# A hybrid encoder trunk on one core: blocks on TensorE, row-mode switches in the queue model, and new ranks

## The chip, the cores and the metric

One Trainium2 chip, one of its cores. The metric is the device time of one execution in microseconds (us). TensorE is called PE here, its weight loads PEld, VectorE DVE, ScalarE ACT, GpSimd POOL and SyncE SP, as in the profile. Smaller is better.

## The reference

Two layers over a sequence of 512 positions of width 1024, all in float32:

```
h = rmsnorm(x, g_attn[l]);  proj = h @ w_in[l]            # 1024 -> 2304 columns
# group A: 8 query heads, 2 key/value heads of 64, window +/-128, a learned sink logit per head
# group B: 4 differential heads, two q/k halves of 64, values of 128:
#          w = softmax(q1 k1) - lam * softmax(q2 k2);  yb = rmsnorm(w @ v) * (1 - lambda_init)
# every q/k head: rmsnorm over the head, then rotary
x = x + concat(ya, yb) @ w_out[l]
h = rmsnorm(x, g_ffn[l]);  gate, val = split(h @ w_up[l])  # 2 x 2816
gate = centred_dwconv(gate, conv_w[l], conv_b[l])          # width 3
x = x + (silu(gate) * val) @ w_down[l]
```

## The kernel before, in words

**Products.** A float32 product is made of three matmuls in a faster 32-bit format: each operand is split into a high part (a cast) and a low part (operand minus high part), and high x high, high x low and low x high are added up in PSUM. `mm3` makes such a triple product. Weights come from HBM in units of 512 KB or less (`wr`), ACT makes the high part (`wh`), DVE the low part (`wl`); there are two raw and three high and low buffers.

**A layer.** `filler` gives PE its large work in this order: projections of group A (`pj_akv`, `pj_aq`), of group B's first half (`pj_bq`, `pj_bk`), both value chunks (`pj_bv`), group B's second half, then the output projection: `out_pass` 0 for group A's part, `out_pass` 1 for group B's first half (`wo`, 512 columns wide), `out_last` twice for its second half (`wo`, 256 wide, one for each half of the positions), then the feed-forward part (`up`, `dn`). Beside it run the attention chains. Group A, for each of 8 tiles: scores `sc_a`, masked maximum and exponential (`so_a`), transposes `pt_a`, their split into `p_a`, product with the values `pv_a`. Group B, for each of 16 tiles named b(layer)_(head)_(query block): six score matmuls `sc_b` of 64 rows each, two heads' halves side by side; maximum `mx_b` on DVE over both; two exponentials `e_b` on ACT; reciprocal, factor and combination `e_b` on DVE; four transposes `wt_b`; split into `wh_b` and `wl_b`; twelve matmuls `yb` for two tiles of a head; after two heads the norm: square `sq_yb` (ACT), column sums `ss_yb` (PE), `rr_yb` (DVE, then a power on POOL), broadcast back by `rt_yb` (PE), `y_yb` (DVE), and the split `yh_b`, `yl_b` that the output projection reads. The scores have one double bank (`sc`), the projections two banks (`mm`).

**What sets the order.** Each piece of work is a generator, a *track*, which yields one operation at a time. `Machine.run` keeps a model of the engines: when each is free, when each operand is there (`Op.cost` has the assumed durations). Of all tracks' next operations it takes, engine by engine, those that could start within a hold time of the earliest, and of these the one with the smallest rank; that one is issued. So the order of the instructions on each engine is fixed when the program is built, and ranks decide between operations that are ready at about the same time: small ranks first, the filler 1000. Ranks touched here: the weight loads, casts and splits (`RK["w"]`, by whether 0, 1 or more units are ready), the evacuation of projection banks (3), q/k norm and rotary tracks of group A (5 and 6) and B (`RK["qkb"]`), the attention tiles of A (10 and up) and B (30 and up), the residual adds behind the output projection (4).

On the chip every engine works through its list in order; an instruction whose operand is late holds up all behind it. All instructions carry the line of the one helper that issues them (L230 before, L247 after), so they are told apart by the names of their tiles.

Of the kernel before, what the change touches and what calls it, by code (L numbers as in the profile page):

```python
# [35 lines left out]
NEAR = {"PE": 0.3, "POOL": 0.079}  # L36
LO_CUT = 2
# [4 lines left out]
RK = {"w": (1, 5, 49), "qkb": (7, 38)}  # L42


class Op:


    def __init__(self, eng, name, args, kw):
# [9 lines left out]
        self.port = False  # L58
        self.pitch, self.lag = self.cost(writes, reads)

    def cost(self, writes, reads):
        n = max([free_size(v) for v in writes[:1]] + [free_size(v) for v in reads])
        if self.eng == "PE":
            if self.name == "transpose" or free_size(writes[0]) <= P:
                return 0.111, 0.165
            n = free_size(writes[0])
            if reads[0].dtype == F32:
                return 4 * n / 2400 + 0.014, 0.165
            half = reads[0].partition_size() == HD
            return (n / 2400 + 0.0135) / (2 if half else 1), 0.165  # L70
# [19 lines left out]
        return 0.33, 0.0  # L90

# [38 lines left out]
class Machine:  # L130
# [3 lines left out]
    def __init__(self, nc):  # L134
        self.raw = {"PE": nc.tensor, "DVE": nc.vector, "ACT": nc.scalar, "POOL": nc.gpsimd, "SP": nc.sync}
# [11 lines left out]
    def tag(self, name, bufs):  # L147
        self.cap[name], self.live[name], self.slots[name] = bufs, 0, [0.0] * bufs

    def got(self, tag, tile_):  # L150
        self.live[tag] += 1
        assert self.live[tag] <= self.cap[tag], tag
        self.mem[tile_.tensor.name] = {"base": heapq.heappop(self.slots[tag])}
        return tile_

    def drop(self, tag, tile_):
        self.live[tag] -= 1
        m = self.mem.pop(tile_.tensor.name)
        heapq.heappush(self.slots[tag], max([m["base"]] + [t for k, v in m.items() if k != "base" for t in v[:2]]))
# [18 lines left out]

    def ready(self, op):
        t = 0.0  # L180
        for name, where in op.reads:
            m = self.mem.get(name)
            if m is None:
                continue
            t = max(t, m["base"])
            for k, (w, r, e) in m.items() if len(m) > 1 else ():
                pass
        return t
# [22 lines left out]
    def put(self, op, start):  # L211
        end = start + op.pitch + op.lag
# [18 lines left out]
        self.log.append((op.eng, start, op.pitch, op.name, op.writes[0][0]))  # L231
# [42 lines left out]
def kernel(  # L274
# [48 lines left out]
    def any_bank(name, tags):  # L323
        tag = min((t for t in tags if m.live[t] < m.cap[t]), key=lambda t: m.slots[t][0])
# [220 lines left out]
    def layer(l, norm):  # L545
# [70 lines left out]
        def qk_track(nm, tag, bank, tp, tab, dst, rq, rank, is_kv=False):  # L616
# [10 lines left out]
            m.spawn(3, go())  # L627

        def qk_out(nm, raw_t, sq_t, tp, tab_i, dst, rq, is_kv):
# [75 lines left out]
        def akv_done(tag, bank, tp):  # L705
            qk_track("ka", tag, bank, tp, 1, [v.unsqueeze(1) for v in ka], None, 5, True)

        def proj_a(i, tags):
            rq = lambda tp: rqa[:, 2 * tp:2 * tp + 2, 2 * i:2 * i + 2, :].rearrange("p t a b -> p t (a b)")
            yield from project(f"aq{i}", lambda tag, bank, tp: qk_track(  # L710
                f"qa{i}", tag, bank, tp, 0, qa[i], rq(tp), 6), tags)
# [14 lines left out]
        a_rank = {s: 10 + i for i, s in enumerate(a_seq)}  # L726
        b_rank = {s: 30 + i for i, s in enumerate(b_seq)}
        a_so = {}

        def a_scores(ip, qb):  # L730
# [9 lines left out]
            for i in range(2):  # L740
                yield m.room("sc")
                scp = new("sc", f"sc_{nm}_{i}")
                sc = (scp[:, 0], scp[:, 1])
                for j, (u, v) in enumerate(((0, 0), (0, 1), (1, 0))):
                    for g in range(2):
                        rs = slice(g * HD, (g + 1) * HD)
                        yield pe.matmul(sc[g][:, :n], lhsT=q[u][rs, i, qb * P:(qb + 1) * P],
                                        rhs=k[v][rs, kb0 * P:kb1 * P], start=j == 0, stop=j == 2)
# [42 lines left out]
        def a_values(ip, qb):  # L791
# [492 lines left out]
```

## Time and profile before

| | us |
|---|---|
| median of 3 runs (lowest, highest) | 1299.78 (1298.53, 1299.89) |
| the profiled execution | 1298.52 |
| its span, first to last instruction | 1296.7 |
| PE busy | 1241.0 |
| DVE, ACT, POOL busy | 756.3, 563.5, 216.9 |

The span runs through attention of layer 0 (to about 294 us), its feed-forward part (to about 650), attention of layer 1 (to about 930) and its feed-forward part. In the view by stretches, each row has the stretch, its length, and for every engine busy time and number of instructions; then the share of PE's full clock that was granted, the share of the DMA engines and GB/s. In a timeline row stand the start, the length, engine, line, operation, out<-in, and in brackets the idle time just before it with what ended it.

### The profile page before, as it was taken

The numbers are of one execution on the slowest core, as the hardware profiler recorded it, in microseconds if no ns is written. First come the engines' busy times: TensorE is split into PE (matmuls) and PEld (weight loads), VectorE is DVE, ScalarE is ACT, GpSimd is POOL, SyncE is SP. The second block draws the span as 40 slices with busy tenths as digits, with TensorE's granted clock in tenths as the row PEclk, the third lists the DMA queues.
The fourth block names the chain that finished last, engine by engine and source line by source line (L and its number), as shares of the span: only waits on it lengthen the run. The fifth ranks groups of instructions, "written<-read, shape, count | busy, mean of one in ns | idle before, by whom it ended". The sixth has DMA issues, their size and how long they took to land.

```text
span 1296.7 us, 17153 instructions
## 1 busy us (share of the span) xinstructions
PE 1241.0 (96%) x6644; PEld 1041.4 (80%) x6644; DVE 756.3 (58%) x1337; ACT 563.5 (43%) x979; POOL 216.9 (17%) x278
## 2 busy tenths in 40 slices
PE   8999899879999999999999999997799999999998
PEld 7987686667888888888898888775688888888887
DVE  6777677647555335554458777876555553355532
ACT  5467664425433223333445776444443332233321
POOL 2450052001111000110243503320011110011100
PEclk8999899879999999999999999998799999999999
DMA  6221121102332333332332211210133323332232
GB/s 206 66 66 34 33 66 51 48 1 84 100 95 91 94 105 98 98 98 75 104 106 66 66 50 50 66 49 18 33 98 97 98 78 98 114 94 94 91 106 91
DMA packets 33617, 102.93 MB, mean 79 GB/s; under 512 B 3968, under 2 KB 5248, under 8 KB 33536
## 3 DMA queue, kind: packets, MB, share of 16 engines
q1 hardware_dynamic: 33536, 101.84, 25.5%
q8 instruction: 52, 0.85, 0.3%
q14 instruction: 29, 0.24, 0.1%
HBM read 99.73 MB, written 2.10 MB: 79 GB/s over the span
## 4 chain that ended last, share of the span: by engine, by line
PE 86%; DVE 7%; ACT 3%; issue 2%; POOL 1%; DMA 0%; SPq 0%; ACTq 0%; DVEq 0%; POOLq 0%
PE up L230 36%; PE dn L230 18%; PE wo L230 5%; PE pj_aq L230 4%; PE pj_bq L230 3%; PE pj_bv L230 3%; PE pj_bk L230 2%; PE pv_a L230 2%; PE sc_b L230 2%; PE yb L230 2%; PE pj_akv L230 2%; PE sc_a L230 2%; PE pt_a L230 1%; DVE wl L230 1%; DVE mx_b L230 1%
## 5 line engine op out<-in xcount | busy, mean ns | idle before, releaser
L230 ACT CAST wh<-wr 128x1024 fp32r<-128x1024 f32 (+2 forms) x202 | 195.3, 967 | 391.4 <-PE up L230 176.6
L230 DVE TENSOR_TENSOR wl<-wr,wh 128x512 fp32r<-128x512 f32 (+3 forms) x248 | 230.6, 944 | 104.5 <-ACT wh L230 103.9
L230 PE MATMUL up<-nf_l,wh 128*128 128x512 f32 x704 | 274.1, 389 | 1.7 <-DVE nf_l L230 1.7
L230 PE MATMUL up<-nf_h,wh 128*128 128x512 f32 x704 | 274.3, 390 | 0.0
L230 PE MATMUL up<-nf_h,wl 128*128 128x512 f32 x704 | 274.1, 389 | 0.0
L230 PE MATMUL dn<-act,wh 128*128 128x512 f32 x704 | 216.8, 389 | 0.0
L230 PEld LDWEIGHTS up<-nf_l,wh 128*128 128x128 f32 x704 | 132.2, 188 | 29.7 <-DVE nf_l L230 2.4
L230 PEld LDWEIGHTS up<-nf_h,wh 128*128 128x128 f32 x704 | 132.2, 188 | 27.8 <-ACT nf_h L230 0.5
L230 PEld LDWEIGHTS dn<-act,wh 128*128 128x128 f32 x704 | 132.2, 188 | 27.4
L230 PEld LDWEIGHTS up<-nf_h,wl 128*128 128x128 f32 x704 | 132.2, 188 | 27.2
L230 POOL TENSOR_TENSOR cv<-cv,rb 128x512 f32<-128x512 f32 x44 | 57.3, 1302 | 525.8 <-ACT cv L230 525.8
L230 PE MATMUL dn<-act,wl 128*128 128x512 f32 x352 | 136.9, 389 | 0.0
L230 DVE TENSOR_TENSOR gp<-up,rb 128x512 f32<-128x512 f32 x44 | 30.5, 693 | 110.4 <-PE up L230 105.0
L230 DVE TENSOR_TENSOR cv<-cv,up 128x512 f32<-128x512 f32 x44 | 30.3, 688 | 90.0 <-POOL gp L230 81.4
L230 PEld LDWEIGHTS dn<-act,wl 128*128 128x128 f32 x352 | 66.1, 188 | 13.7
L230 DVE SCALAR_TENSOR_TENSOR cv<-gp,cols,cv 128x512 f32<-128x512 f32 x88 | 65.9, 749 | 7.0 <-ACT cv L230 2.5
L230 DVE TENSOR_TENSOR x<-x,dn 128x512 f32<-128x512 f32 x32 | 22.0, 688 | 74.1 <-PE dn L230 74.1
L230 ACT ACTIVATE e_b<-sc_b,mx_b,rqb 128x512 f32<-128x512 f32 x64 | 49.5, 776 | 34.1 <-DVE mx_b L230 31.6
L230 ACT ACTIVATE cv<-cv 128x512 f32<-128x512 f32 x44 | 27.8, 632 | 82.0 <-DVE cv L230 82.0
L230 DVE TENSOR_TENSOR x<-x,wo 128x512 f32<-128x512 f32 (+1 forms) x64 | 34.9, 551 | 18.2 <-PE wo L230 17.6
L230 DVE TENSOR_REDUCE mx_b<-sc_b 128x2 f32<-128x1024 f32 x32 | 39.1, 1221 | 10.8 <-PE sc_b L230 10.7
L230 ACT ACTIVATE so_a<-so_a,ng_a,rqa 128x256 f32<-128x256 f32 (+1 forms) x64 | 41.3, 650 | 3.6 <-DVE ng_a L230 3.5
(202 smaller groups left out, 2330.0 us busy)
## 6 DMA issues: line engine op xcount, KB each, us to landing
wr<-w_up SPq DMA_DIRECT2D x88, 512.0 KB, 3.6
wr<-w_in SPq DMA_DIRECT2D x34, 512.0 KB, 3.7
wr<-w_down SPq DMA_DIRECT2D x32, 384.0 KB, 3.0
wr<-w_down SPq DMA_DIRECT2D x32, 320.0 KB, 2.9
wr<-w_out SPq DMA_DIRECT2D x16, 512.0 KB, 3.7
x<-xT SPq DMA_DIRECT2D x8, 256.0 KB, 4.4
outT<-x SPq DMA_DIRECT2D x8, 256.0 KB, 2.0
prob_f<-w_in SPq DMA_DIRECT2D x8, 128.0 KB, 4.3
```

The costliest lines, as they stand in the source:

```text
L230: getattr(self.raw[op.eng], op.name)(*op.args, **op.kw)
```

## The change

It leaves every computation as it is, and does four things:

1. `Batch`: a group of PE operations that is yielded and issued as one, without others in between. The three matmuls of a triple product, the six scores of a tile (of A and of B), the transposes of a tile and the small products of the norm become such groups.
2. The model of PE: a matmul of 64 rows after one of 128 rows, or the other way round, now costs a switch (`SWITCH`: 0.2 into 64-row mode, 0.085 out of it); float32 products of 128 columns or fewer cost 0.222 and not 0.111; the time from an operand to PE goes from 0.3 to 0.2.
3. The ranks are set anew: group A's tiles from 10 to 39 and up, A's query track from 6 to 36, its key track from 5 to 2, group B's first half from 7 to 36 and second from 38 to 2, adds of the two output passes from 4 to 400, evacuations from 3 to 4, the norm of B four ranks behind its tile, weights with one unit ready from 5 to 28, with more from 49 to 400.
4. `LO_CUT` 2 to 1: the low parts of input and output projection weights are one operation of 1024 columns instead of two of 512.

```diff
-NEAR = {"PE": 0.3, "POOL": 0.079}
-LO_CUT = 2
+SWITCH = {True: 0.2, False: 0.085}
+NEAR = {"PE": 0.2, "POOL": 0.079}
+LO_CUT = 1
...
-RK = {"w": (1, 5, 49), "qkb": (7, 38)}
+RK = {"w": (1, 28, 400), "qkb": (36, 2), "x": 400, "xl": 4, "a": 39, "b": 30, "evac": 4, "qka": 36, "kv": 2,
+      "bn": 4, "nsq": 21, "av": -2, "bv": 0}
...
+class Batch:
+    def __init__(self, ops):
+        self.ops = ops
+        self.eng, self.port = "PE", False
+        self.reads = [r for o in ops for r in o.reads]
+        self.writes = [w for o in ops for w in o.writes]
+        self.pitch = sum(o.pitch for o in ops)
+        self.half = ops[0].half
...
     def put(self, op, start):
+        if isinstance(op, Batch):
+            for v in op.ops:
+                self.put(v, start)
+                start = self.free["PE"]
+            return
+        if op.eng == "PE" and op.half != self.half:
+            self.free["PE"] += SWITCH[op.half]
+            start += SWITCH[op.half]
+            self.half = op.half
...
     def mm3(acc, a, b, start, stop):
-        yield pe.matmul(acc, lhsT=a[0], rhs=b[0], start=start, stop=False)
-        yield pe.matmul(acc, lhsT=a[0], rhs=b[1], start=False, stop=False)
-        yield pe.matmul(acc, lhsT=a[1], rhs=b[0], start=False, stop=stop)
+        yield Batch([pe.matmul(acc, lhsT=a[0], rhs=b[0], start=start, stop=False),
+                     pe.matmul(acc, lhsT=a[0], rhs=b[1], start=False, stop=False),
+                     pe.matmul(acc, lhsT=a[1], rhs=b[0], start=False, stop=stop)])
...
-        a_rank = {s: 10 + i for i, s in enumerate(a_seq)}
-        b_rank = {s: 30 + i for i, s in enumerate(b_seq)}
+        a_rank = {s: RK["a"] + i for i, s in enumerate(a_seq)}
+        b_rank = {s: RK["b"] + i for i, s in enumerate(b_seq)}
...
+            ops = []
             for n, (u, v) in enumerate(((0, 0), (0, 1), (1, 0))):
                 for c in range(2):
                     rs = slice(c * HD, (c + 1) * HD)
-                    yield pe.matmul(scp[:, c], lhsT=q[u][rs, j, qb * P:(qb + 1) * P], rhs=k[v][rs, j, :],
-                                    start=n == 0, stop=n == 2)
+                    ops.append(pe.matmul(scp[:, c], lhsT=q[u][rs, j, qb * P:(qb + 1) * P], rhs=k[v][rs, j, :],
+                                         start=n == 0, stop=n == 2))
+            yield Batch(ops)
...
-                m.spawn(4, add_x(d, tag, acc, slice(0, S)))
+                m.spawn(RK["x"], add_x(d, tag, acc, slice(0, S)))
```

What this makes of the order, at three places. (In the names, `sc_b0_0_0` is the scores of layer 0, head 0, query block 0, and `yb0_1_1` the weighted values of layer 0, half 1, second pair of query blocks; `wo0_2_0_4` is the last output product of layer 0, first half of the positions, fifth block of rows. The number at a name's end tells buffers apart.)

PE, the scores of group B's first tile in layer 0, before:

```order
L230 MATMUL pv_a0_1_2_1829<-p_a0_1_2_1_1801,va0_89 128x512 x3
L230 MATMUL sc_b0_0_0_1834<-bkh0_0_677,bqh0_0_675 128x512
L230 MATMUL pv_a0_1_2_1829<-p_a0_1_2_2_1828,va0_89 128x512
L230 MATMUL sc_b0_0_0_1834<-bkh0_0_677,bqh0_0_675 128x512
L230 MATMUL sc_b0_0_0_1834<-bkl0_0_678,bqh0_0_675 128x512 x2
L230 MATMUL sc_b0_0_0_1834<-bkh0_0_677,bql0_0_676 128x512
L230 MATMUL pv_a0_1_2_1829<-p_a0_1_2_2_1828,va0_89 128x512 x2
L230 MATMUL sc_b0_0_0_1834<-bkh0_0_677,bql0_0_676 128x512
```

and now:

```order
L247 MATMUL pt_a0_1_2_2_1739<-ident_74,so_a0_1_2_1_1_1478 128x128
L247 MATMUL sc_b0_0_0_1762<-bkh0_0_677,bqh0_0_675 128x512 x2
L247 MATMUL sc_b0_0_0_1762<-bkl0_0_678,bqh0_0_675 128x512 x2
L247 MATMUL sc_b0_0_0_1762<-bkh0_0_677,bql0_0_676 128x512 x2
L247 MATMUL pv_a0_1_2_1757<-p_a0_1_2_0_1721,va0_89 128x512 x3
```

The six scores stand together; before, products of group A stood between them.

PE, the last norm of layer 0's attention, before:

```order
L230 MATMUL yb0_1_1_2963<-wh_b0_3_2_2999,vb0_1_1_1680 128x256
L230 MATMUL ss_yb0_1_1_3073<-unit_78,sq_yb0_1_1_3067 128x1 x4
L230 MATMUL rt_yb0_1_1_3081<-ident_74,rr_yb0_1_1_3078 128x128 x4
L230 MATMUL wo0_2_1_0_3089<-yh0_b1_2912,wh24_2622 128x256 x2
L230 MATMUL wo0_2_1_0_3089<-yh0_b1_2912,wl24_2641 128x256 x2
```

and now:

```order
L247 MATMUL wo0_2_0_4_3017<-yh0_b1_2879,wh25_2839 128x256
L247 MATMUL ss_yb0_1_1_3015<-unit_78,sq_yb0_1_1_3001 128x1 x4
L247 MATMUL wo0_2_0_4_3017<-yh0_b1_2879,wh25_2839 128x256
L247 MATMUL wo0_2_0_4_3017<-yh0_b1_2879,wl25_2844 128x256 x2
L247 MATMUL wo0_2_0_4_3017<-yl0_b1_2880,wh25_2839 128x256 x2
L247 MATMUL wo0_2_0_5_3033<-yh0_b1_2879,wh25_2839 128x256 x2
L247 MATMUL wo0_2_0_5_3033<-yh0_b1_2879,wl25_2844 128x256 x2
L247 MATMUL wo0_2_0_5_3033<-yl0_b1_2880,wh25_2839 128x256 x2
L247 MATMUL wo0_2_0_6_3041<-yh0_b1_2879,wh25_2839 128x256 x2
L247 MATMUL rt_yb0_1_1_3031<-ident_74,rr_yb0_1_1_3024 128x128 x4
L247 MATMUL wo0_2_0_6_3041<-yh0_b1_2879,wl25_2844 128x256 x2
```

Products of the first half of the positions (`wo0_2_0`) stand between the links of the norm; before, they were all done by then.

DVE, the last tile's softmax of layer 0, before:

```order
L230 TENSOR_REDUCE mx_b0_3_3_3006<-sc_b0_3_3_2982 128x2
L230 TENSOR_TENSOR x5_71<-x5_71,wo0_2_0_5_3008 128x256
L230 TENSOR_TENSOR x6_72<-x6_72,wo0_2_0_6_3021 128x256
L230 TENSOR_TENSOR wl_b0_3_2_3000<-wt_b0_3_2_3001,wh_b0_3_2_2999 128x4x128
L230 TENSOR_TENSOR x7_73<-x7_73,wo0_2_0_7_3030 128x256
L230 SCALAR_TENSOR_TENSOR mx_b0_3_3_3006<-mx_b0_3_3_3006,rqb0_87 128x2
L230 RECIPROCAL rl_b0_3_3_3043<-bl0_1_1_2790 128x1
L230 TENSOR_SCALAR al_b0_3_3_3045<-bl0_1_1_2790,rl_b0_3_3_3043,nlam0_85 128x1
L230 SCALAR_TENSOR_TENSOR e_b0_3_3_0_2926<-e_b0_3_3_1_2927,al_b0_3_3_3045,e_b0_3_3_0_2926 128x512
```

and now:

```order
L247 TENSOR_REDUCE mx_b0_3_3_2917<-sc_b0_3_3_2892 128x2
L247 SCALAR_TENSOR_TENSOR mx_b0_3_3_2917<-mx_b0_3_3_2917,rqb0_87 128x2
L247 TENSOR_TENSOR x5_71<-x5_71,wo0_1_5_2889 128x512
L247 TENSOR_TENSOR wl_b0_3_2_2909<-wt_b0_3_2_2910,wh_b0_3_2_2908 128x4x128
L247 TENSOR_TENSOR x6_72<-x6_72,wo0_1_6_2922 128x512
L247 RECIPROCAL rl_b0_3_3_2944<-bl0_1_1_2679 128x1
L247 TENSOR_SCALAR al_b0_3_3_2952<-bl0_1_1_2679,rl_b0_3_3_2944,nlam0_85 128x1
L247 SCALAR_TENSOR_TENSOR e_b0_3_3_0_2853<-e_b0_3_3_1_2854,al_b0_3_3_2952,e_b0_3_3_0_2853 128x512
```

The scaled maximum, which the exponentials on ACT wait for, now follows its reduction at once; the residual adds (`x`) and the low part `wl_b` come behind it. The adds are those of the second output pass (`wo0_1`), where before they were those of the last.

More of the change, by code (lines that the diff above doesn't have):

```diff
@@ L58, in __init__ @@
         self.port = False
+        self.half = False
         self.pitch, self.lag = self.cost(writes, reads)
@@ L134, in __init__ @@
     def __init__(self, nc):
+        self.half = False
+        self.heir = {}
         self.raw = {"PE": nc.tensor, "DVE": nc.vector, "ACT": nc.scalar, "POOL": nc.gpsimd, "SP": nc.sync}
@@ L158, in drop @@
         m = self.mem.pop(tile_.tensor.name)
-        heapq.heappush(self.slots[tag], max([m["base"]] + [t for k, v in m.items() if k != "base" for t in v[:2]]))
+        last = max([m["base"]] + [t for k, v in m.items() if k != "base" for t in v[:2]])
+        heapq.heappush(self.slots[tag], (last, tile_.tensor.name))
     def room(self, tag, n=1, under=None):
@@ L177, in step @@
             self.tracks.remove(t)
[L179 to L188, printed above, removed]
     def when(self, op):
@@ L230, in put @@
         getattr(self.raw[op.eng], op.name)(*op.args, **op.kw)
-        self.log.append((op.eng, start, op.pitch, op.name, op.writes[0][0]))
+        self.log.append((op.eng, start, op.pitch, op.name, op.writes[0][0], op))
     def run(self):
@@ L683, in qk_out @@
             tr = trt[:, :nb * CW].rearrange("p (b q) -> p b q", b=nb)
-            for b in range(nb):
-                for i in range(2):
-                    yield pe.transpose(tr[:, b, i * P:(i + 1) * P], raw[:, i, b * P:(b + 1) * P], ident)
+            yield Batch([pe.transpose(tr[:, b, i * P:(i + 1) * P], raw[:, i, b * P:(b + 1) * P], ident)
+                         for b in range(nb) for i in range(2)])
             m.drop("rp", raw_t)
@@ L705, in akv_done @@
         def akv_done(tag, bank, tp):
-            qk_track("ka", tag, bank, tp, 1, [v.unsqueeze(1) for v in ka], None, 5, True)
+            qk_track("ka", tag, bank, tp, 1, [v.unsqueeze(1) for v in ka], None, RK["kv"], True)
         def proj_a(i, tags):
@@ L800, in a_values @@
                 tr = new("at", f"pt_{nm}_{b}")
-                for g in range(2):
-                    for i in range(2):
-                        o = (2 * g + i) * P
-                        yield pe.transpose(tr[:, o:o + P], so[2 * i + g][:, b * P:(b + 1) * P], ident)
+                yield Batch([pe.transpose(tr[:, (2 * g + i) * P:(2 * g + i + 1) * P],
+                                          so[2 * i + g][:, b * P:(b + 1) * P], ident) for g in range(2) for i in range(2)])
                 yield m.room("prob")
@@ L905, in b_weights @@
             tr = new("at", f"wt_b{l}_{h}_{qb}")
-            for b in range(NT):
-                yield pe.transpose(tr[:, b * P:(b + 1) * P], w[:, b * P:(b + 1) * P], ident)
+            yield Batch([pe.transpose(tr[:, b * P:(b + 1) * P], w[:, b * P:(b + 1) * P], ident) for b in range(NT)])
             m.drop("tmp", w)
@@ L948, in b_norm @@
             ss = new("tq", f"ss_{nm}")
-            for i in range(4):
-                yield pe.matmul(ss[:, i:i + 1], lhsT=sq[:, i * P:(i + 1) * P], rhs=ones, start=True, stop=True)
+            yield Batch([pe.matmul(ss[:, i:i + 1], lhsT=sq[:, i * P:(i + 1) * P], rhs=ones, start=True, stop=True)
+                         for i in range(4)])
             m.drop("tmp", sq)
@@ L958, in b_norm @@
             rt = new("tq", f"rt_{nm}")
-            for i in range(4):
-                yield pe.matmul(rt[:, i * P:(i + 1) * P], lhsT=rr[:, i:i + 1].broadcast_to([P, P]), rhs=ident,
-                                start=True, stop=True)
+            yield Batch([pe.matmul(rt[:, i * P:(i + 1) * P], lhsT=rr[:, i:i + 1].broadcast_to([P, P]), rhs=ident,
+                                   start=True, stop=True) for i in range(4)])
             yield dve.tensor_tensor(out=y[:, :S], in0=y[:, :S], in1=rt, op=ALU.mult)
@@ L1014, in all_values @@
                     if j:
-                        m.spawn(b_rank[half, qb, j], b_norm(half, qb // 2))
+                        m.spawn(b_rank[half, qb, j] + RK["bn"], b_norm(half, qb // 2))
         def proj_b(half):
@@ L1082, in add @@
                         yield from nf.add(d)
-                m.spawn(4, add())
+                m.spawn(RK["xl"], add())
             if half:
```

31 lines of the change are left out of this document (17 added, 14 removed).

## The prediction

> **What bounds the kernel now.** I read the page's span first, then busy time by stretch, then TensorE's own timeline where it pauses.
>
> ```profile
> span 1296.7 us, 17153 instructions
> core 0: us, PE busy (x) PEld busy (x) DVE busy (x) ACT busy (x) POOL busy (x), PEclk, DMA share, GB/s
> 400.00:450.00 50.00, 50.00 (x222) 41.44 (x221) 21.78 (x28) 15.93 (x20) 4.09 (x9) 1.00 0.30 91
> ...
> 118.00:142.00 24.00, 17.77 (x102) 13.73 (x101) 16.66 (x51) 16.95 (x41) 1.27 (x1) 0.86 0.15 45
> 242.00:294.00 52.00, 37.92 (x209) 32.19 (x209) 27.65 (x59) 20.13 (x39) 2.02 (x2) 0.74 0.04 10
> 750.00:850.00 100.00, 99.02 (x666) 83.57 (x664) 79.10 (x176) 63.59 (x140) 25.86 (x21) 1.00 0.18 55
> 854.00:930.00 76.00, 60.54 (x325) 48.96 (x324) 44.63 (x90) 29.77 (x58) 3.02 (x3) 0.80 0.08 22
> ```
>
> TensorE (PE) is the bound, and in the feed-forward part (400 to 450 us) nothing can be won: 50.00 of 50 busy at full clock. The attention of a layer is different. Its ends (242 to 294 us, 854 to 930 us) and one place in layer 0 (118 to 142 us) are idle for 14.1, 15.5 and 6.2 us, and there the granted clock falls to 0.74, 0.80 and 0.86, so that busy PE is slow too. Lost time is idle plus (1 - clock) x length: 14.1 + 13.5 = **27.6**, 15.5 + 15.2 = **30.7**, 6.2 + 3.4 = **9.6 us**. The row 750 to 850 us is the counterexample: the same attention, VectorE (DVE) at 79%, and PE loses 1 us in 100. So an attention stage can run nearly full if enough independent work stands between the links of its chains.
>
> What the ends wait for, on PE alone:
>
> ```profile
> 245.40 0.50 PE L230 MATMUL sc_b<-bkh,bqh 64*128 64x512 f32 x2 [3.17 <-ACT e_b L230]
> ...
> 273.63 0.63 PE L230 MATMUL wt_b<-ident,e_b 128*128 128x128 f32 x4 [3.69 <-DVE e_b L230]
> 279.12 1.86 PE L230 MATMUL ss_yb<-unit,sq_yb 128*128 128x1 f32 x8 [0.75 <-ACT sq_yb L230]
> 282.33 2.07 PE L230 MATMUL rt_yb<-ident,rr_yb 128*128 128x128 f32 x8 [1.34 <-POOL rr_yb L230]
> 285.90 0.79 PE L230 MATMUL wo<-yh_b,wh 128*128 128x256 f32 x2 [1.50 <-ACT yh_b L230]
> ...
> 294.07 0.40 PE L230 MATMUL up<-nf_h,wh 128*128 128x512 f32 x1
> ```
>
> One chain, link after link: scores, softmax, transposes, weighted values, norm (ss_yb, rt_yb), last output product. Every link has an idle time in brackets because no other PE work is left. Layer 1 ends with the same instructions.
>
> **The change, part by part.** Every edit moves instructions; both programs have 6,556 matmuls. Two terms come from that.
>
> *Ends of the layers.* I count by the two orders, each matmul at the pitch of its rows (0.227 us for 512 columns, 0.12 for 256, 0.11 for a transpose, score pairs 0.23). From the scores of tile b0_2_2 (the row at 245.40) to the first up product stand 24.3 us of work before: 24 scores, 20 transposes, 36 yb, 16 products of ss and rt in two passes each, 96 last-output products. The trace took 48.7 us for it, plus the 3.17 us wait. In the changed order the same stretch holds also 48 output products of 512 columns: **35.2 us**. From b1_2_0 (854.36 us) it is 42.5 before and **56.9 us** now (57 such products and 12 yb more). So 10.9 and 14.4 us of other work have moved behind the start of the chain.
>
> From below: if the chain takes as long as now, only this moved work is hidden, 10.9 + 14.4 = 25.3 us won. From above: all of 27.6 + 30.7 = 58.3. Which is nearer? From 245.40 to 285.90 the chain takes 40.5 us, of which some 11 are the clock (13.5, less 2.5 for the 5 us of last products that also ran slow) and 2 are DVE's queue (below): 27.5 us at full clock, against 35.2 less 5.8 for the last 48 products, so 29.4 us of PE work now between the same links. They balance, so I stand near the upper bound, less what single links still lack:
>
> ```profile
> 245.96 0.40 PE L230 MATMUL sc_b<-bkh,bql 64*128 64x512 f32 x2
> 246.55 1.22 DVE L230 TENSOR_REDUCE mx_b<-sc_b 128x2 f32<-128x1024 f32 x1
> 249.11 0.78 ACT L230 ACTIVATE e_b<-sc_b,mx_b,rqb 128x512 f32<-128x512 f32 x1
> 250.52 0.75 DVE L230 SCALAR_TENSOR_TENSOR e_b<-e_b,al_b,e_b 128x512 f32<-128x512 f32 x1
> ...
> 266.26 0.40 PE L230 MATMUL sc_b<-bkh,bql 64*128 64x512 f32 x2
> 267.36 1.22 DVE L230 TENSOR_REDUCE mx_b<-sc_b 128x2 f32<-128x1024 f32 x1
> 270.31 0.15 DVE L230 SCALAR_TENSOR_TENSOR mx_b<-mx_b,rqb 128x2 f32<-128x2 f32 x1
> 272.73 0.75 DVE L230 SCALAR_TENSOR_TENSOR e_b<-e_b,al_b,e_b 128x512 f32<-128x512 f32 x1
> ```
>
> From the last score pair's pitch to the weights' transposes a free chain needs 5.1 us (246.2 to 251.3); with residual adds queued between its DVE steps it needed 7.0 (266.5 to 273.5). In the changed order the 16 tiles of a layer have 4.6 to 13.6 us of PE work there, most 4.8 to 6.9. Against 5.1 us the shortfalls add to 1.2 us per layer, against 7.0 to some 15.6. The other links now have more than they need: scores to the next scores 3.4 us or more (needed: about 3.7, the second exponential's row ends at 249.9), yb to ss_yb 0.96 or more (0.75), ss_yb to rt_yb 1.56 or more (1.34); only rt_yb to the last output product, 1.20, is short of 1.50. I take 7 us left per layer: nearer to the free chain, because of the row 750 to 850 us, but not at it, since DVE is dense there (first rival). Term: -58.3 + 14 = **-44.3**.
>
> [...]
>
> ```profile
> 24.56 0.38 PE L230 MATMUL pj_aq<-wh,na_h 128*128 128x256 f32 x1 [2.13 <-ACT wh L230]
> 26.09 0.41 PE L230 MATMUL pj_aq<-wh,na_h 128*128 128x256 f32 x1
> 26.30 0.41 PE L230 MATMUL pj_aq<-wl,na_h 128*128 128x256 f32 x1
> ```
>
> After 2.13 us of waiting the pitch is 0.21 instead of 0.12, so short pauses are not free, and I keep the 7.
>
> *Scores in one block.* A 64-row score matmul beside full ones costs at each crossing:
>
> ```profile
> 146.12 0.49 PE L230 MATMUL sc_b<-bkh,bqh 64*128 64x512 f32 x1
> 146.55 0.50 PE L230 MATMUL pv_a<-p_a,va 128*128 128x512 f32 x1
> ...
> 238.30 0.50 PE L230 MATMUL sc_b<-bkh,bqh 64*128 64x512 f32 x2
> 238.63 0.40 PE L230 MATMUL sc_b<-bkl,bqh 64*128 64x512 f32 x2
> 238.87 0.40 PE L230 MATMUL sc_b<-bkh,bql 64*128 64x512 f32 x2
> 239.20 0.50 PE L230 MATMUL wo<-yh_b,wl 128*128 128x512 f32 x1
> 239.53 0.40 PE L230 MATMUL wo<-yh_b,wh 128*128 128x512 f32 x1
> 239.77 0.39 PE L230 MATMUL wo<-yl_b,wh 128*128 128x512 f32 x1
> ```
>
> Inside the block a pair follows after 0.24 us (238.63 to 238.87), as one full product follows another (239.53 to 239.77). But the first pair takes 0.33, the last pair 0.33 until the full product starts, and that one 0.33 again: 0.09 three times, and a fourth time at the entry, some 0.4 us a block, 0.2 a crossing. The orders have 160 crossings before and 128 now: 32 x 0.2 = 6.4 us. A lone score takes a whole step for half a pair's work (146.12 to 146.55); 14 times before, never now: 14 x 0.115 = 1.6. Nothing hides PE's own time, so it is 8.0 at most; at least nothing, if the splits only filled waits. Some splits do stand beside the place at 118 to 142 us. Term: **-6**. Keeping transposes and triple products together wins nothing by itself: their pitch is the same alone or in a row. It costs, if one of a block's operands is late, and the block waits at its head; that belongs to the leftovers.
>
> *Place in layer 0, 118 to 142 us.*
>
> ```profile
> 131.38 2.26 PE L230 MATMUL pt_a<-ident,so_a 128*128 128x128 f32 x8 [3.78 <-ACT so_a L230]
> ```
>
> Group A's transposes wait for a softmax. From a tile's scores to its first transposes the old order has 9.0 us of PE work at the long wait; the new one has 12.6 there, and 8.8 at least in any tile. The long wait should go, with the slow clock behind it: 9.6 less 2.6 that stay, **-7.0** (from 0 to 9.6).
>
> *Start.* The transposes of the first keys stood behind the first group-A projections and now stand in the middle of them, about 5.4 us of PE work earlier, while on DVE only one weight split and a few small steps have gone from in front of them. They may wait 0 to 2.5 us: **+1.5**.
>
> *Whole instead of halved low weight parts.* 100 halves (96 on DVE) become 50 whole operations on DVE:
>
> ```profile
> 243.54 1.22 DVE L230 TENSOR_TENSOR wl<-wr,wh 128x1024 fp32r<-128x1024 f32 x1
> L230 DVE TENSOR_TENSOR x<-x,dn 128x512 f32<-128x512 f32 x32 | 22.0, 688 | 74.1 <-PE dn L230 74.1
> ```
>
> A whole one takes 1.22 us, two operations of half the width 2 x 0.69, so the work does not grow; what queues behind one waits up to 0.6 us longer, hidden where PE has the links covered, and up to 24 x 0.6 = 14 us a layer where not, which is inside the 15.6. The order of feed-forward work is the same on DVE.
>
> **Sum.** -44.3 - 6 - 7.0 + 1.5 = -55.8 on the span: 1240.9. The profiled run took 1298.5 for a span of 1296.7, so 1.8 around it: **1243 us**. (The median of the runs, 1299.8, is 1.3 above this one run.) Ends: with the low bounds of all terms 25.3 + 0 + 0 - 2.5 is won, 1276; with the high ones 58.3 + 8.0 + 9.6, 1223.
>
> **Rivals.**
>
> *VectorE becomes the bound of the ends.* From the maximum of tile b0_3_0 to that of b0_3_3 the new DVE order holds 5 maxima and 3 weight splits at 1.22 us, 5 combinations at 0.75, 17 adds, low parts and norm steps at 0.69, and some 18 small ones at 0.15: 28 us, against 26.9 us of PE work. For: that is over 100%, and each maximum behind a 1.22 us split delays a score bank of which there is one. Against: the 79% of the row 750 to 850 us, and that after this stretch little DVE work follows. The leftover would be 16 instead of 7 a layer: 1261.
>
> *The waits only move.* The blocks wait at their heads as the old pieces did, and only the crossings are saved: 1292. Against it stands the counted 25.3 us of cover.
>
> *Slower: weights come late.* With one unit ready, its casts and splits had rank 5 and now 28, behind evacuations and projections' norms. Each of the 36 input chunks that is late costs 2.7 us (the row at 24.56 and its 0.55 after it). From 21 late chunks on, the change loses; with 30 it is 1243 + 81 = 1324. Against: after the first chunks no projection row before shows such a wait, and rank 28 is still ahead of both attentions' 30 to 46.
>
> **Chances.** Forecast 0.72, VectorE 0.17, moved waits 0.06, late weights 0.05. The likeliest's own range is 1231 to 1255; with VectorE's case the range is 1233 to 1268. About 0.2% (2.6 us) is what a measurement of this kernel can tell from no change: faster 0.94, same 0.02, slower 0.04.
>
> **What would show it.** Right: the rows for the last 50 us of each layer's attention show PE over 90% busy at a clock of 0.95 or more, the last wt_b waits under 1.5 us instead of 3.69, the norm's links wait under 0.5, the pause at 131 us is gone, all 64 score blocks stand six in a row. Wrong: clock rows below 0.9 at both ends and DVE busy over 90% there (VectorE), brackets "<-DVE wl" or "<-ACT wh" on projections (weights), or the same idle sum elsewhere in the attention (moved).

## The result, and the profile after

The changed kernel takes **1226.64 us** (median of 4 runs, 1225.53 to 1226.96) against 1299.84 for the kernel before beside it: ratio 0.9434, 95% interval 0.9418 to 0.9450. It is 73 us faster; 57 were forecast (1243), and the time lies below the range of 1233 to 1268. The direction and the main places were right, the size was not.

The page of the changed kernel, its span, busy time and the clock in 40 slices:

```profile
span 1224.9 us, 17089 instructions
...
PE 1206.8 (99%) x6644; PEld 1018.1 (83%) x6644; DVE 746.5 (61%) x1291; ACT 561.2 (46%) x979; POOL 215.0 (18%) x274
...
PEclk9999999999999999999999999999999999999999
```

Of the 71.8 us by which the span is shorter, PE's idle time gave 37.6 (1296.7 - 1241.0 = 55.7 before, 1224.9 - 1206.8 = 18.1 now) and its busy time 34.2: the same matmuls, run at a granted clock of 0.998 instead of 0.972 and with fewer row-mode crossings (changes between 64-row and 128-row matmuls: 128 by the orders, 160 before). The stretches that answer to those of the forecast (the end of layer 0's attention is now at 215 to 254 us, that of layer 1 at 795 to 858):

```profile
core 0: us, PE busy (x) PEld busy (x) DVE busy (x) ACT busy (x) POOL busy (x), PEclk, DMA share, GB/s
118.00:142.00 24.00, 24.00 (x180) 21.08 (x178) 17.67 (x47) 18.24 (x44) 0.00 (x0) 1.00 0.26 81
...
215.00:254.00 39.00, 37.88 (x254) 32.06 (x254) 32.21 (x62) 19.53 (x37) 2.02 (x2) 1.00 0.14 41
...
795.00:858.00 63.00, 61.90 (x389) 50.40 (x388) 51.03 (x97) 31.71 (x62) 3.02 (x3) 1.00 0.14 43
```

Both ends run at 97 to 98% busy with a clock of 1.00, where they had 73 and 80% with 0.74 and 0.80. VectorE is busy for 83% of the end of layer 0 (32.21 of 39) and is not the bound. What is left of pauses of over 0.15 us on PE in the last 33 us before the up products of either layer, from its timeline:

```profile
238.20 0.63 PE L247 MATMUL wt_b<-ident,e_b 128*128 128x128 f32 x4 [0.16 <-DVE e_b L247]
240.06 0.50 PE L247 MATMUL wo<-yh_b,wh 128*128 128x256 f32 x2 [0.51 <-DVE x L247]
248.27 0.50 PE L247 MATMUL wo<-yh_b,wh 128*128 128x256 f32 x2 [0.31 <-ACT yh_b L247]
...
844.09 0.50 PE L247 MATMUL wo<-yh_b,wh 128*128 128x256 f32 x2 [0.51 <-DVE x L247]
852.28 0.50 PE L247 MATMUL wo<-yh_b,wh 128*128 128x256 f32 x2 [0.32 <-ACT yh_b L247]
```

The last transposes wait 0.16 us instead of 3.69, the last output product 0.31 instead of 1.50, and the norm's links not at all.

By stage, from the starts of the first instructions of each stage in both traces: attention of layer 0 gained 39.6 us, its feed-forward part 1.4, attention of layer 1 30.3, its feed-forward part 0.4. From the scores of b0_2_2 to the first up product it now takes 39.4 us for 35.2 of counted work (4.2 lost; before, with the wait ahead of these scores, 51.8 for 24.3), and from b1_2_0 62.9 for 56.9 (6.0 lost; before 75.5 for 42.5). So the ends lost 27.5 and 33.0 us before, and lose 4.2 and 6.0 now.

### The profile page after: what moved, and what is told of

Its sections match the earlier page's. It is cut to its first block, busy times and chain, and to the rows that moved or that the text cites. A ratio compares the mean times of both kernels' runs of the same rounds, so it can differ in the third digit from the quotient of the medians.

```text
span 1224.9 us, 17089 instructions
## 1 busy us (share of the span) xinstructions
PE 1206.8 (99%) x6644; PEld 1018.1 (83%) x6644; DVE 746.5 (61%) x1291; ACT 561.2 (46%) x979; POOL 215.0 (18%) x274
## 4 chain that ended last, share of the span: by engine, by line
PE 88%; DVE 5%; ACT 3%; issue 2%; POOL 0%; DMA 0%; SPq 0%; ACTq 0%; POOLq 0%; DVEq 0%
PE up L247 38%; PE dn L247 20%; PE wo L247 5%; PE pj_aq L247 4%; PE pj_bq L247 4%; PE pj_bv L247 3%; PE pj_bk L247 2%; PE pv_a L247 2%; PE sc_b L247 2%; PE yb L247 2%; DVE wl L247 1%; PE sc_a L247 1%; PE pt_a L247 1%; PE pj_akv L247 1%; PE wt_b L247 1%
## 5 line engine op out<-in xcount | busy, mean ns | idle before, releaser
L247 DVE TENSOR_TENSOR wl<-wr,wh 128x1024 fp32r<-128x1024 f32 (+2 forms) x202 | 228.2, 1130 | 100.7 <-ACT wh L247 99.9
L247 PEld LDWEIGHTS dn<-act,wh 128*128 128x128 f32 x704 | 132.1, 188 | 27.5
L247 DVE TENSOR_TENSOR cv<-cv,up 128x512 f32<-128x512 f32 x44 | 30.3, 688 | 88.1 <-POOL gp L247 80.2
L247 ACT CAST wh_b<-wt_b 128x512 fp32r<-128x512 f32 x32 | 18.8, 586 | 45.0 <-PE wt_b L247 45.0
```

The lines of the kernel that those rows point to most:

```text
L247: getattr(self.raw[op.eng], op.name)(*op.args, **op.kw)
```

## The experiments

Three theories were put to the chip. **Cover** is the forecast's: a link of a chain (scores to weights' transposes above all) needs a fixed time, and PE pauses where the order has less other work between its two ends (its cover); what the order lacks, added up over all links, is the loss. The price in the expectations, 1.1 us of time for 1 us lacking, is a ratio taken from the kernel before, not a term worked out from a mechanism. **Blocks**: the gain is that scores stand together, and ranks only move waits. **VectorE**: its sum of work is what limits the attention.

### Which part of the change does it

`ranks_old` takes the ranks out of the changed kernel:

```diff
-RK = {"w": (1, 28, 400), "qkb": (36, 2), "x": 400, "xl": 4, "a": 39, "b": 30, "evac": 4, "qka": 36, "kv": 2,
-      "bn": 4, "nsq": 21, "av": -2, "bv": 0}
+RK = {"w": (1, 5, 49), "qkb": (7, 38), "x": 4, "xl": 4, "a": 10, "b": 30, "evac": 3, "qka": 6, "kv": 5,
+      "bn": 0, "nsq": 21, "av": -2, "bv": 0}
```

> The changed kernel with the ranks of before: blocks, queue model and whole low parts stay. Theory (cover): the gain is TensorE work that stands behind the start of a layer's last chains, so that single links no longer wait. By this kernel's order the links from a tile's last score pair to its weights' transposes lack 18.6 us in layer 0 and 23.2 us in layer 1 of the 5.1 us each needs (20.6 and 30.5 before, 2.0 and 2.0 in the changed kernel); at 1.1 us of time for 1 us lacking, about the ratio of before, it is 1226.6 + 1.1 x 37.8 = 1268, up to 1276 if the pause at 118 to 142 us of before is back too. Rival (blocks): the gain is that scores stand in blocks and nothing splits them, and the ranks only move waits: 1230 to 1240.

Measured 1271.6 us (ratio to before 0.977, 0.974 to 0.979). The 18.6 and 23.2 us in the expectation do not come out for the one link that it names: counted on the trace at the forecast's pitches, the links from scores to transposes, at 5.1 us each, lack 7.6 and 10.0 us. They may be sums over several links; the record does not say.

`model_old` takes the queue model out:

```diff
-SWITCH = {True: 0.2, False: 0.085}
-NEAR = {"PE": 0.2, "POOL": 0.079}
+SWITCH = {True: 0.0, False: 0.0}
+NEAR = {"PE": 0.3, "POOL": 0.079}
...
-            if self.name == "transpose":
+            if self.name == "transpose" or n <= P:
                 return 0.111, 0.165
             if reads[0].dtype == F32:
-                return 2 * max(4 * n / 2400 + 0.014, 0.111) if n > P else 0.222, 0.165
+                return 4 * n / 2400 + 0.014, 0.165
```

The edit also takes back the doubled cost of float32 products of more than 128 columns, which the list of the change does not name.

> The changed kernel with the queue model of before (no price for a row-mode switch, the old operation costs, nearness 0.3); blocks, new ranks and whole low parts stay. 128 crossings; the links lack 11.0 and 13.8 us, 20.8 more than in the changed kernel; 32.5 and 46.4 us of work stand in the ends. Cover: 1226.6 + 1.1 x 20.8 = 1249. If the model's costs only rename times and ranks and blocks do all: 1226 to 1232.

Measured 1247.6 (0.960, 0.957 to 0.963). `blocks_only` has both edits and keeps only blocks and whole low parts:

> Blocks and whole low parts as in the changed kernel; ranks, operation costs and the missing row-mode switch of the queue model as before. Cover: the links lack 29.2 and 19.1 us, 44.3 more than in the changed kernel: 1226.6 + 1.1 x 44.3 = 1275, up to 1283 with the pause at 118 to 142 us. Blocks: 1230 to 1240, since every block is there and the crossings are the same 128.

Measured 1283.7 (0.986, 0.983 to 0.989). `no_blocks` turns every block into single steps, and `ranks_only` does this too and has the old queue model and `LO_CUT = 2`:

```diff
-        yield Batch([...])
+        yield from [...]
```

> The changed kernel with every block undone: ranks, queue model with its row-mode switches and whole low parts stay. 160 crossings and 18 lone scores. Cover: the links lack 4.7 and 9.9 us, 10.6 more than in the changed kernel: 1226.6 + 11.7, and 32 crossings x 0.2 + 18 x 0.115 = 8.5: 1247. Blocks: 1285 to 1300.

Measured 1248.7 (0.958, 0.956 to 0.961).

> The kernel before with the new ranks alone: no block, old queue model, halved low parts. 154 crossings between 64-row and 128-row products and 18 lone scores. Cover: the links lack 9.9 and 15.2 us, 21.1 more than in the changed kernel, 26 crossings x 0.2 and 18 x 0.115 more: 1226.6 + 23.2 + 5.2 + 2.1 = 1257. Blocks: the ranks only move waits, 1285 to 1300.

Measured 1265.4 (0.972, 0.968 to 0.975). In `score_blocks_undone` only the scores of A and B lose their blocks:

```diff
-                yield Batch(ops)
+                yield from ops
```

> The changed kernel with only the score blocks undone; transposes, triple products and norm sums stay together, ranks and queue model stay. 156 crossings, 14 lone scores; the links lack 8.6 and 5.7 us. Cover and crossings: 1226.6 + 1.1 x 10.3 + 28 x 0.2 + 14 x 0.115 = 1245, of it 7 on TensorE's own time and 11 in waits. If crossings are free: 1238. If the blocks of the other operations do the work: 1230 or less.

Measured 1250.2 (0.961, 0.958 to 0.964). Cover forecast 1268 to 1276, 1249, 1275 to 1283, 1247, 1257 and 1245 for these six, and the chip gave 1271.6, 1247.6, 1283.7, 1248.7, 1265.4 and 1250.2. The largest miss, 8 us with the ranks alone, is a place that I had left out there: the pause at 118 to 142 us is back (3.78 us at 131.00), with the clock at one half from 132 to 139 and from 142 to 146 us. Blocks as the sole cause has fallen: with all blocks and the old ranks and model 1.4% are won, some 18 us, with the ranks alone 2.8% or 37. All of the blocks' worth is in the score blocks (22.0 us for all, 23.6 for these, whose four runs spread from 1247.2 to 1253.7). Taken out one by one, ranks, blocks and model are worth 45, 22 and 21 us, more than the 73 of all, so they overlap, as they would if a link that one of them leaves short is short whatever the others do.

### What a crossing costs

`blocks_split` keeps the order of the changed kernel and issues the last pair of every score block one full product later:

```diff
+        if self.hold:
+            self.held.append(op)
+            return
...
+        self.issue(op)
+        if op.eng == "PE":
+            self.flush()
```

> The changed kernel with its own order on every engine, except that the last pair of each of the 64 score blocks is issued one full product later, alone between two 128-row instructions: 256 crossings instead of 128, and no matmul more. Price as in the forecast (0.2 us a crossing): 128 x 0.2 = 25.6 more, 1252. If a crossing costs nothing and the splits of before only filled waits: 1227 to 1231, for the later last pair alone (0.23 us later in the links).

Measured 1249.2 (0.960, 0.958 to 0.962): 22.6 us for 128 crossings, **0.18 us each** in the whole and, by the timeline of PE below, 0.2 on the spot. PE's busy time grew by 23.2 us (1206.8 to 1230.0) and its idle time did not (18.1 and 17.3), so this is PE's own time and not a wait in the links.

```profile
159.62 0.28 PE L221 MATMUL pj_bq<-wh,na_l 128*128 128x256 f32 x1
159.83 0.50 PE L221 MATMUL sc_b<-bkh,bqh 64*128 64x512 f32 x2
160.17 0.40 PE L221 MATMUL sc_b<-bkl,bqh 64*128 64x512 f32 x2
160.50 0.39 PE L221 MATMUL pj_bq<-wh,na_h 128*128 128x256 f32 x1
160.81 0.49 PE L221 MATMUL sc_b<-bkh,bql 64*128 64x512 f32 x2
161.24 0.39 PE L221 MATMUL pj_bq<-wl,na_h 128*128 128x256 f32 x1
161.46 0.28 PE L221 MATMUL pj_bq<-wh,na_l 128*128 128x256 f32 x1
```

From 159.62 to 161.46 stand six scores and three products, 1.84 us. The changed kernel, unsplit, has six scores and two products from the start of the first to that of the last of these rows of its timeline:

```profile
160.26 0.28 PE L247 MATMUL pj_bk<-wh,na_l 128*128 128x256 f32 x1
160.47 0.50 PE L247 MATMUL sc_b<-bkh,bqh 64*128 64x512 f32 x2
160.80 0.40 PE L247 MATMUL sc_b<-bkl,bqh 64*128 64x512 f32 x2
161.04 0.39 PE L247 MATMUL sc_b<-bkh,bql 64*128 64x512 f32 x2
161.36 0.39 PE L247 MATMUL pj_bk<-wh,na_h 128*128 128x256 f32 x1
161.58 0.28 PE L247 MATMUL pj_bk<-wl,na_h 128*128 128x256 f32 x1
```

That is 1.32 us, and a third product's pitch is 0.12: 0.40 us for two more crossings.

### What stands inside a link, and what beside it

`adds_early` changes one rank of the changed kernel, so that residual adds run on VectorE as soon as they can:

```diff
-RK = {..., "x": 400, ...}
+RK = {..., "x": 4, ...}
```

> The changed kernel with the residual adds at rank 4, as before, instead of 400: they stand again between the steps of the softmax on VectorE. By the order the links lack 13.3 us in each layer (2.0 in the changed kernel), and 29.1 and 54.6 us of TensorE work stand in the ends (35.2 and 56.9). Cover: 1226.6 + 1.1 x 22.6 = 1251, with PE pauses before weights' transposes of over 1.2 us and half-clock windows at both ends. If the place of the adds is nothing by itself: under 1232.

Measured 1253.7 (0.964, 0.961 to 0.967), as cover says, with half-clock windows at both ends (the granted clock is 0.90 from 203 to 258 us and 0.97 from 763 to 863). `max_twice` issues the maximum of each group-B tile twice:

```diff
         getattr(self.raw[op.eng], op.name)(*op.args, **op.kw)
+        if op.eng == "DVE" and op.name == "tensor_reduce" and "sc_b" in op.reads[0][0]:
+            getattr(self.raw[op.eng], op.name)(*op.args, **op.kw)
```

> The changed kernel with the maximum over each group-B score tile taken twice on VectorE (the second writes the same): 64 x 1.22 us more on VectorE, the order of all engines is the same otherwise. It lengthens the link from scores to weights' transposes to 6.3 us and that from scores to the next scores to 4.9. Cover: by the order the links then lack 24.8 us instead of 4.0: 1226.6 + 1.1 x 20.8 = 1249. If VectorE is close to being the bound of the ends (the forecast's first rival): it is over 95% busy there and the time above 1265. If the links have slack that the order does not show: under 1235.

The count in it is wrong: group B has 32 tiles, not 64. Measured 1260.8 (0.970, 0.967 to 0.973), between the two expectations and 12 us above cover's. By the pages VectorE's busy time grew by 35.5 us (746.5 to 782.0) and the time by 34.1, 0.96 us for each us, although VectorE is not full. One stretch of attention in layer 1, in the changed kernel and here, and two pauses of PE at the end of layer 0 here:

```profile
763.00:863.00 100.00, 96.97 (x614) 79.44 (x613) 84.36 (x152) 55.05 (x106) 23.51 (x18) 1.00 0.17 51
...
763.00:863.00 100.00, 87.79 (x553) 69.75 (x553) 85.61 (x139) 50.82 (x102) 29.02 (x23) 1.00 0.15 47
```

```profile
239.34 0.50 PE L247 MATMUL wo<-yh_b,wh 128*128 128x512 f32 x1 [1.47 <-DVE x L247]
246.15 0.39 PE L247 MATMUL yb<-wl_b,vb 128*128 128x256 f32 x1 [1.25 <-DVE wl_b L247]
```

VectorE is at 86% (84 in the changed kernel) and PE at 88% (97): the pauses sit before many different instructions, also at links that I had not counted (a bank that waits for its residual add, weighted values that wait for a low part). In this run an operation put into VectorE's list delayed what stood behind it, and the order leaves the links next to no reserve. The second maximum stands inside the link, so this run does not part VectorE's load from the place of the work; no run puts the same 1.22 us behind the link. `combine_out` goes the other way and leaves out the operation that subtracts the second softmax of each tile, so this part of the result is missing:

```diff
-        getattr(self.raw[op.eng], op.name)(*op.args, **op.kw)
+        if not (op.eng == "DVE" and op.name == "scalar_tensor_tensor" and op.writes[0][0].startswith("e_b")):
+            getattr(self.raw[op.eng], op.name)(*op.args, **op.kw)
```

> The changed kernel without the operation on VectorE that combines the two exponentials of a group-B tile (32 x 0.75 us), so its second softmax is left out of the result; the order is the same otherwise. Taking the maximum twice (32 operations of 1.22 us) cost 34 us, 0.88 us for each us of VectorE. If VectorE binds in both directions, 24 us less work on it would give up to 21: 1206. If the order of the changed kernel has TensorE at its own floor, only the pauses left in the attention can go, at most 1.1 + 1.7 + 3.0 + 1.7 us of the stretches from 142 to 258 and 720 to 863: about 1220.

Measured 1224.6 (0.942, 0.939 to 0.945): 22.5 us less work on VectorE give 2 us. So VectorE limits in one direction only. With this order PE is close to its own floor (99% busy); a delay in a link shows, and relief hardly does.

What was then still open is why a loaded link cost so little in the changed kernel. Its timeline of VectorE at the last tile of layer 0, whose last score pair starts at 232.83 us:

```profile
233.63 1.22 DVE L247 TENSOR_REDUCE mx_b<-sc_b 128x2 f32<-128x1024 f32 x1
234.88 0.16 DVE L247 SCALAR_TENSOR_TENSOR mx_b<-mx_b,rqb 128x2 f32<-128x2 f32 x1
234.96 0.68 DVE L247 TENSOR_TENSOR x<-x,wo 128x512 f32<-128x512 f32 x1
235.55 0.68 DVE L247 TENSOR_TENSOR wl_b<-wt_b,wh_b 128x512 fp32r<-128x512 f32 x1
236.15 0.68 DVE L247 TENSOR_TENSOR x<-x,wo 128x512 f32<-128x512 f32 x1
...
237.30 0.75 DVE L247 SCALAR_TENSOR_TENSOR e_b<-e_b,al_b,e_b 128x512 f32<-128x512 f32 x1
```

Three operations of 0.68 us run while ScalarE computes the two exponentials, in time that the chain spends waiting anyway; from the last score pair's pitch (233.06) to the end of the combination (238.05) it takes 5.0 us, as a free chain (5.1 in the forecast). In the kernel before, the same kinds of operation stood one place earlier:

```profile
267.36 1.22 DVE L230 TENSOR_REDUCE mx_b<-sc_b 128x2 f32<-128x1024 f32 x1
268.49 0.81 DVE L230 TENSOR_TENSOR x<-x,wo 128x256 f32<-128x256 f32 x2
269.22 0.68 DVE L230 TENSOR_TENSOR wl_b<-wt_b,wh_b 128x512 fp32r<-128x512 f32 x1
269.98 0.42 DVE L230 TENSOR_TENSOR x<-x,wo 128x256 f32<-128x256 f32 x1
270.31 0.15 DVE L230 SCALAR_TENSOR_TENSOR mx_b<-mx_b,rqb 128x2 f32<-128x2 f32 x1
272.22 0.16 DVE L230 RECIPROCAL rl_b<-bl 128x1 f32<-128x1 f32 x1 [1.76 <-ACT e_b L230]
```

Here the scaling of the maximum comes 1.7 us late, the exponentials with it, and VectorE then idles for 1.76 us. The other tiles show the same pattern. In the changed kernel four tiles a layer have less than 5.1 us of cover (4.6 to 5.0), and in each of them the scaling starts within 0.04 us of the maximum's end. In the six where it comes 0.5 to 1.8 us late, the cover is 5.7 us or more. `one_between` puts just one operation back into that place and changes nothing else: the scaling is held and issued behind the next operation on VectorE.

```diff
+        if op.eng == "DVE" and op.name == "scalar_tensor_tensor" and op.writes[0][0].startswith("mx_b"):
+            self.held.append(op)
+            return
```

> The changed kernel with one exchange on VectorE in each of the 32 group-B tiles: the operation that stood behind the scaling of the maximum (a residual add, a low part, ...; 0.17 to 1.22 us, most 0.68) now stands between the maximum and its scaling. No operation more; TensorE's order and all covers are the same. If what counts is what stands inside a link (the forecast's 5.1 against 7.0), each tile's weights come about 0.7 us later; over the reserve that the trace of the changed kernel shows at each tile (0.05 to 0.94 us) this is 4.9 us a layer: 1226.6 + 9.8 = 1236. If only VectorE's sum of work counts: 1226 to 1228.

Measured 1235.4 (0.950, 0.947 to 0.952). It is as the place says (1236), with the same work on every engine. `links_free_old_ranks` does the reverse under the old ranks:

```diff
...
-            yield dve.tensor_reduce(out=mx, in_=scp, axis=AX, op=ALU.max)
-            yield dve.scalar_tensor_tensor(out=mx, in0=mx, scalar=-1.0, in1=rq, op0=ALU.mult, op1=ALU.mult)
+            yield Batch([dve.tensor_reduce(out=mx, in_=scp, axis=AX, op=ALU.max),
+                         dve.scalar_tensor_tensor(out=mx, in0=mx, scalar=-1.0, in1=rq, op0=ALU.mult, op1=ALU.mult)])
```

> The changed kernel with the ranks of before, and the maximum of a group-B tile and its scaling issued as one block on VectorE, so that no add or split stands between them. By the order the links lack 19.0 and 18.8 us of cover (18.6 and 23.2 with the old ranks alone, which took 1271.6). If cover decides: 1226.6 + 1.1 x 33.8 = 1264. If the operations inside the link were the larger part of the loss: under 1250.

Measured 1257.4 (0.968, 0.964 to 0.971), 14 us below `ranks_old`. Its order is planned anew too, and by the counts cover gives 4 of the 14. So, by that count, some 10 of the 45 us that the ranks are worth lie in what stands inside the links; with the links free and the old cover, 31 us are still missing.

### A better version

The start still had two pauses and a half-clock window in the changed kernel:

```profile
24.42 0.38 PE L247 MATMUL pj_aq<-wh,na_h 128*128 128x256 f32 x1 [1.56 <-ACT wh L247]
25.68 0.58 PE L247 MATMUL pj_aq<-wl,na_h 128*128 128x256 f32 x1 [0.88 <-DVE wl L247]
```

The chunk is there, but its cast stands on ScalarE behind an evacuation that waits 3.81 us for a power on GpSimd (done at 22.11 us). `cast_first` moves cast and low part of this one chunk ahead of it, by holding what stood between and issuing it behind them:

```diff
+        unit = any(name.startswith("wr") for name, _ in op.reads)
+        if op.eng in self.units and unit:
+            self.units[op.eng] += 1
+        if self.units.get(op.eng) == 1 and not unit:
+            self.held[op.eng].append(op)
+            return
```

> The changed kernel with one step moved on two engines: the cast of the second full weight chunk on ScalarE and its low part on VectorE come before the evacuation of the first group-A projection, for which ScalarE idles 3.81 us. TensorE's order is the same. The pauses of 1.56 and 0.88 us at 24.4 us of the changed kernel and the half-clock window behind them (25.4 to 28.8) should go: 2.4 + 1.7 = 4.1 us, 1222.5. Rival: TensorE then comes early to the third chunk, whose low part VectorE ends only at 34.5 us, or to the first keys' transposes, and waits there instead: 1226 to 1228, with the half-clock window a little later.

> The changed kernel itself, beside the next three on the same chip: 1226 to 1228.

Measured 1223.5 (1222.83 to 1224.15) against 1226.9 (1225.21 to 1227.64) for the changed kernel on the same chip, 3.3 us or 0.27% less, with ranges that do not meet; to the kernel before 0.941 (0.939 to 0.944). Its timeline of ScalarE, where the two casts now stand together, and the pauses that are left on PE between 20 and 30 us:

```profile
16.87 2.06 ACT L221 CAST wh<-wr 128x1024 fp32r<-128x1024 f32 x2
```

```profile
21.33 0.39 PE L221 MATMUL pj_aq<-wl,na_h 128*128 128x256 f32 x1 [0.46 <-DVE wl L221]
28.32 0.41 PE L221 MATMUL tr_ka<-ident,raw_ka 128*128 128x128 f32 x2 [0.37 <-issue]
33.35 0.41 PE L221 MATMUL tr_ka<-ident,raw_ka 128*128 128x128 f32 x2 [0.31 <-DVE raw_ka L221]
```

Of the 4.1 us expected 3.3 came. The rival is right to a part: the second transposes of keys now wait 0.31 us for their operand, and the first come 0.1 us after theirs is written, though the bracket there names no wait.

The 1.7 us for the slow clock came only in part of the executions. The same two pauses (1.56 and 0.88 us in one, 1.54 and 0.88 in the other) stand in both profiled executions of the changed kernel, the first of which has a window of half clock behind them and the second none:

```profile
22.01:25.42 3.41, 1.24 (x9) 0.83 (x7) 1.50 (x2) 3.23 (x7) 1.64 (x4) 1.00 0.47 154
...
20.40:23.81 3.41, 1.82 (x14) 1.41 (x12) 1.12 (x2) 1.83 (x4) 3.04 (x4) 1.00 0.48 148
23.81:27.23 3.42, 2.13 (x15) 1.94 (x16) 2.95 (x8) 3.06 (x7) 1.19 (x2) 1.00 0.27 52
```

The stretches are steps of 3.41 us, counted on from the clock records of each execution. In the first (`after`) one step holds the whole long pause, and PE is busy for 1.24 of 3.41 us; in the second (`after_again`) the steps fall so that the pauses spread over two, PE is busy for 1.82 and 2.13 us in them, and the clock stays full. The spans are 1224.9 and 1223.4, against 1221.8 for `cast_first`: 3.1 us less where the clock had fallen, 1.6 where it had not.

## Why the prediction was wrong in size, step by step

The forecast's span was 1240.9 and 1224.9 was measured. Of these 16.0 us:

- **Ends of the layers: 6.0.** The mechanism is right: the work counted behind the start of the last chains hides their waits, and idle time and slow clock went together. Wrong is the step "I take 7 us left per layer". Lost are 4.2 and 6.0 us, and of that the blocks' own crossings are 4 x 0.4 and 8 x 0.4 (the score blocks of the two stretches), so 2.6 and 2.8 are left: 5.4 instead of 14, which is 8.6 less. The two ends have the same number of crossings before (8 and 16), so on the same count they lost 27.5 + 33.0 - 4.8 = 55.7 us there, and not the 58.3 that the forecast started from: 50.3 were won at the ends where it had 44.3. That its 58.3 came so near is partly luck: idle time plus (1 - clock) x length counts an idle us at half clock as 1.5 us, some 5 us too much at the two ends, and leaves out the shorter delays that the count takes in. Between a free link (1.2 us a layer lacking) and a loaded one (15.6) I stood in the middle, as if VectorE's load and PE's cover were independent. One planner sets both: where the cover is short (4.6 to 5.0 us) the link was free, and operations stood where the chain waits for ScalarE. `one_between` shows the price of the place, 8.8 us for one operation moved by one position in 32 tiles.
- **The clock.** I kept the 7 because "short pauses are not free". At the size of the pauses that were left (0.16 to 0.51 us in the ends) they cost no more than themselves: the clock stayed at 1.00, and also in `max_twice`, which pauses for a good part of its 34 us in pieces of up to 1.5 us. The last section has the sizes at which it fell.
- **Place in layer 0: 2.6.** I left 2.6 of the 9.6 us; the row of 118 to 142 us is full, so all 9.6 went.
- **Start: 1.5.** The transposes of the first keys were to wait up to 2.5 us. They follow without a pause at either place:

```profile
32.08 0.38 PE L247 MATMUL tr_ka<-ident,raw_ka 128*128 128x128 f32 x2
...
36.61 0.41 PE L247 MATMUL tr_ka<-ident,raw_ka 128*128 128x128 f32 x2
```

- **Scores in one block: 1.3.** With the price that `blocks_split` measures, 32 x 0.18 to 0.2 and 14 lone scores x 0.115 are 7.3 to 8.0 us; I took 6. Right, slightly small.
- **Pauses of layer 0 that were not counted: 2.2.** The forecast looked at 118 to 142 and at 242 to 294 us only. PE also idled for 3.9 us from 180 to 242 us; the changed kernel idles for 1.7 from 142 us to the start of its end. The kernel before, then the changed one:

```profile
180.00:242.00 62.00, 58.12 (x324) 45.27 (x323) 48.79 (x85) 28.52 (x54) 15.35 (x12) 1.00 0.19 60
...
142.00:215.00 73.00, 71.34 (x472) 59.43 (x470) 60.34 (x106) 42.31 (x87) 28.39 (x22) 1.00 0.17 52
```

- **Feed-forward parts, taken as unchanged: 1.9.** They are 1.4 and 0.4 us shorter. In both, the first products with the low part `nf_l` now wait 0.6 us less for VectorE (in layer 1 0.29 instead of 0.87 us); the small rest stays open.

```profile
299.56 0.50 PE L230 MATMUL up<-nf_l,wh 128*128 128x512 f32 x1 [0.87 <-DVE nf_l L230]
...
258.74 0.50 PE L247 MATMUL up<-nf_l,wh 128*128 128x512 f32 x1 [0.28 <-DVE nf_l L247]
```

These come to 15.5 of the 16.0 us. The account is by count, not by a run for each line, and no run tries the whole low parts alone. One link that the forecast called covered was not quite: scores to the next scores, 3.4 us against 3.7 needed. The changed kernel shows no pause of over 0.1 us there.

Of the rivals, late weights and moved waits have fallen with the traces: waits for a weight of more than 0.2 us stand only in the first 26 us, as before. VectorE as the bound of the ends has fallen as put (no row over 90%), yet it was the nearest to the truth about the risk: `max_twice` shows that a further us inside the links costs 0.96. What I had not seen is that VectorE limits through the place of its operations (8.8 us in `one_between`), also while it is idle for 14% (`max_twice`).

## What to carry to other kernels

Where a chain runs through several engines, count for each link the independent work that the bottleneck has between its two ends, and look at what stands inside the link on the other engines: operations belong in the gaps where the chain waits for a third engine, not before the step that this engine waits for (here 8.8 us for one operation in each of 32 tiles). If one planner places both, look in its order whether the links with short cover are free, as they were here, and then forecast near the free bound. Price mode crossings from the trace; here 128 more of them added 23.2 us to the bottleneck's own busy time, and its idle time stayed (18.1 and 17.3 us).

## What the runs showed of the hardware

In these traces the granted clock is 1.00 or 0.50 and changes in steps of 3.41 us, and in 56 of 58 falls the step before was one in which pauses had left PE busy for less than 0.68. Counted in the clock records and PE's rows of 16 profiled runs, by PE's busy share in the window before, while the clock was full (a window at a bound may fall on either side of it): below 0.53 the next window ran at half clock 37 times of 38; from 0.53 to 0.68 19 times of 48; above 0.68 2 times of some 5,500. Once at half, it came back after no window below 0.83 (54 of them) and after 57 of 62 above. In the kernel before alone these are 6 of 6, 4 of 8, none of 343, none of 11 and 10 of 10. The bounds only sort the windows of these runs; what sets the clock was not shown. Two pairs of neighbouring windows of the kernel before:

```profile
127.37:130.79 3.42, 0.23 (x2) 0.03 (x1) 3.00 (x8) 1.86 (x4) 1.27 (x1) 1.00 0.24 30
130.79:134.20 3.41, 2.23 (x8) 1.54 (x8) 1.84 (x6) 3.41 (x9) 0.00 (x0) 0.50 0.48 168
222.95:226.36 3.41, 2.10 (x13) 1.55 (x13) 3.08 (x5) 1.10 (x2) 2.61 (x3) 1.00 0.01 2
226.36:229.78 3.42, 3.16 (x15) 2.14 (x16) 1.90 (x6) 1.63 (x4) 0.00 (x0) 1.00 0.44 153
```

With 0.23 us busy of 3.42 the next window is at half; with 2.10 of 3.41 (0.61) it stays full. In `max_twice` the attention's windows behind the start (from 30 us on) were never below 0.69 busy, and none of the many pauses there dropped the clock (1.00 from 100 to 258 and from 720 to 863 us). The long slow stretches at the old ends go with the counts of the way back: in the five half-clock windows from 274.15 us of the kernel before PE is busy for 0.76, 0.78, 0.61, 0.56 and 1.00 of each, and only behind the last is the clock full again.
